# One fused transformer layer in float32: the rest of every second weight piece made by ScalarE and an accumulating DMA, and attention on unsplit float32

## The chip, the cores and the metric

The kernel runs on one core of a Trainium2 chip. The metric is the device time of one execution in microseconds (us). The engines are named as the profile names them: PE (TensorE, matrix products; PEld are its weight loads), DVE (VectorE), ACT (ScalarE), POOL (GpSimd) and SP (SyncE, which here only issues DMAs). SBUF is the on-chip memory of 128 partitions, PSUM the banks into which PE writes.

## The reference

One layer for 256 tokens of 2048 features. A mixer has two branches: dilated attention with three groups of 8 heads, and a gated linear attention. Both read one wide product of x; a gated sum of them goes through w_out, then comes a layer norm, a convolutional feed-forward block of 5632 features, and a second layer norm.

```
parts = split(x @ w_in)                       # q, k, v of three groups; gla inputs; gates
for each group: p = softmax(q k^T / sqrt(128) + bias), o = p v     # 8 heads of 128
ya = softmax-weighted sum of the groups' o, @ w_proj_a
yb = (gla(...) normalised * silu(gr)) @ w_proj_b
x  = layernorm(ALPHA x + (sigmoid(m_a) ya + sigmoid(m_b) yb) @ w_out)
h  = silu(conv3(x @ w_gate)) * (x @ w_up)
x  = layernorm(ALPHA x + h @ w_down)
```

All of it is float32, and nearly all of the time is matrix products with weights that are used once.

## The kernel before, in words

The weights come as a stream of pieces, each 128 partitions by 2048 float32 numbers (1 MB), which the host has laid out in the order of use. `piece` (line 135) takes the next one: SP loads it into a tile `raw` (three buffers), ACT copies it into a tile `whi` of type float32r, the main part (line 115), and DVE subtracts to get the rest, `wlo = raw - whi` (line 116); the kernel's comment calls the two exact 12-bit parts. `whi` and `wlo` have two buffers each.

Every product with the weights is made of three of such parts: main by main, main by rest, rest by main. Two forms of product use the pieces. `b_tile` (lines 182 to 189) makes 128 features by 256 tokens: for each of 16 blocks one matmul of 512 columns (line 187, both parts of the tokens against `whi`) and one of 256 (line 188, against `wlo`). `a_chunk` makes 128 tokens by 512 features with three matmuls of 512 columns for each block and half of the tokens (lines 237 to 239). A piece feeds 12288 streamed columns in either form. After a `b_tile`, `b_sum` (ACT line 231, DVE line 232) adds the two halves of the PSUM bank.

The order on each engine is set by a scheduler at build time, which lets ACT, DVE and SP work on pieces ahead of PE as far as the buffers allow. Every engine then executes its own list strictly in order; waits are on semaphores. So what an engine may do early is bounded by its list and by buffers: the next `whi` and `wlo` can be written only when PE has read the piece that held the buffer.

Around the stream the stages are: v, q and k of the attention heads with the attention itself pushed in between (`side`, `pump`), the linear attention's inputs, the linear attention, the projection `yp`, the gates `gr` and `m` with `pb`, `wo` with the first layer norm, and the feed-forward block with `fg` and `fu` (gate and up) and `wd` (down) in three parts of 20, 20 and 4 feature tiles.

Attention works on split operands: q and k are summed into a temporary tile and split (48 times), v is split on its way out of PSUM, and so are the transposed probabilities `pT`. `scores` (line 325) then takes two matmuls per half of the queries and two DVE operations to add the two PSUM halves and the bias; `mix` (line 366) takes four matmuls per group. The bias of a head is loaded by four small DMAs on POOL's queue (line 323) into a tile of the pool `big`, which has 7 buffers.

Of the kernel before, what the change touches and what calls it, by code (L numbers as in the profile page):

```python
# [14 lines left out]
ALU = mybir.AluOpType  # L15
# [22 lines left out]
# columns of w_in  # L38
# [8 lines left out]
# columns of the packed per-partition parameters  # L47
# [10 lines left out]
def hybrid_layer(ctx: ExitStack, tc: tile.TileContext, wp, xt, wgl, gw, par, relb, onehot, ln2, out):  # L58
# [20 lines left out]
    def blk(name, dt=F32):  # L79
        """2 KB of every partition."""  # L80
        n_blk[0] += 1
        return bpool.tile([P, 512], dt, tag="blk", name=f"{name}_{n_blk[0]}", bufs=NBLK)

    def tmp(name, dt=F32):
        """1 KB of every partition."""
        n_blk[0] += 1
        return tpool.tile([P, S], dt, tag="tmp", name=f"{name}_{n_blk[0]}", bufs=NTMP)

    def big(name, shape, dt=F32):
        """3 KB of every partition."""  # L90
        n_blk[0] += 1
        return tpool.tile([P, *shape], dt, tag="big", name=f"{name}_{n_blk[0]}", bufs=7)
# [25 lines left out]
    def piece_in_blocks(i, on_pool=None):  # L118
        """A piece out of turn, or one that leaves the pool's parts to the next."""
# [61 lines left out]
    def b_tile(name, parts, opnd, nk):  # L181
        """[128 features, tokens]: main part in columns :S, the rest in S:."""
# [13 lines left out]
    def b16_three(names, opnd, second):  # L196
        """Three feature tiles side by side, for an operand that is still being made."""
# [15 lines left out]
    def halves(a):  # L213
        return a.rearrange("p (a c) -> p a c", a=2)

    def evacuate(name, pss, parts=False):
        """[tile of tokens], or [tile of tokens][part]"""
        out = []
        for ps in pss:
            if parts:  # L220
                two = blk(name, F32R), blk(name, F32R)
                split(*two, ps)
                out.append(two)
            else:
                out.append(blk(name))
                nc.scalar.activation(out[-1], ps, AF.Copy)
# [14 lines left out]
    def a_chunk(name, opnd, nk, first=None, n_pump=1):  # L241
        """[128 tokens, 512] for both halves of the tokens."""
# [11 lines left out]
    def a_pair_by_half(name, opnd, second):  # L254
        """Two chunks of one piece each: first all of one half of the tokens."""
# [48 lines left out]
    def copies():  # L304
        """Every row once for each of 32 queries, so that a row's start can move with the query."""
# [8 lines left out]
    def attend(h, qk, vs, hp, hv):  # L314
        """Stages of head h: hp its place in its q and k tiles, hv in its v tiles."""
# [10 lines left out]
        def scores(g):  # L326
            def f():
                if not g:
                    st["s"] = blk("s0")[:, :384], big("s1", (768,))
                q, k = (x[hp] for x in qk[g])  # L330
                for t in range(2):
                    n = (t + 1) * P
                    ps = bank("ps")
                    nc.tensor.matmul(ps[:, : 2 * n], q[:, t * P : (t + 1) * P], halves(k)[:, :, :n], start=True, stop=False)
# [18 lines left out]
        def turn(g):  # L353
            def f():
# [6 lines left out]
                p = big("pT", (2, 384), F32R)  # L361
                split(p[:, 0], p[:, 1], pt[:, :384])
# [3 lines left out]
        def mix(g):  # L366
            def f():
                if not g:
                    st["po"] = bank("po")
                po, p = st["po"], st["p", g]  # L370
                v0, v1 = ([a[:, hv * P : (hv + 1) * P] for a in vs[g][t]] for t in range(2))
# [3 lines left out]
                nc.tensor.matmul(po[:, S + P :], v1[1], p[:, 0, S:], start=False, stop=(g == 2))  # L375
                if g == 2:
                    f32 = tmp("yaf")
                    b_sum(po, f32)
                    y = blk("ya", F32R)
                    split(y[:, :S], y[:, S:], f32)  # L380
# [9 lines left out]
    for half in range(2):  # L390
        vs = []
        for g in range(3):
# [5 lines left out]
            vs.append(evacuate("v", pss, parts=True))  # L398
        for pr in range(2):
            qk = []  # L400
            st = [attend(4 * half + 2 * pr + j, qk, vs, j, 2 * pr + j) for j in range(2)]
            for g in range(3):
                two = []
                for which in range(2):
                    hl = []
                    for j in range(2):
                        ps = b16("qk", xop)
                        f = tmp("qkf")
                        b_sum(ps, f)
                        hl.append(blk("qk", F32R))  # L410
                        split(hl[j][:, :S], hl[j][:, S:], f)
                        pump()
                    two.append(hl)
# [18 lines left out]
    # low-rank gate  # L432
# [5 lines left out]
    # both operands of the gate's product three times over, from rows 0, 32 and 64, so that  # L438
    # one pass over the rows sums the products of their parts
# [31 lines left out]
    def gla(h):  # L471
# [33 lines left out]
        def keys():  # L505
# [3 lines left out]
            # groups of two chunks of keys, for the chunks of queries 0 | 1 | 2, 3 | 2 | 3  # L509
# [141 lines left out]
    def residual(d):  # L651
        """ALPHA x, less the centre."""
# [162 lines left out]
NBLK = 38  # L815
NTMP = 14


# [1 line left out]
def _by_rows(w, c, n):  # L820
    """Columns c..c+n of all rows, 128 rows to a partition's place."""
# [46 lines left out]
def _bucket_rows():  # L868
    """One-hot buckets of the distance 255 - j, by group; a last row of -1e30 where it is masked."""
# [62 lines left out]
```

## Time and profile before

| | |
|---|---|
| two timed runs | 1923.16 and 1927.13 us, median 1925.14 |
| the profiled execution | 1924.5 us from its first to its last instruction; no other time is given for it, so what lies around the span is inside the 0.6 us between this and the median |
| granted clock of PE | 0.995 of full speed |
| busy: PE / DVE / ACT / POOL | 99% / 60% / 47% / 5% of the span |
| moved by DMA | 352.6 MB, mean 183 GB/s |

The page has a row per engine with its busy time, forty slices of the span with the busy tenths of each engine, and the chain of work that ended last. A group's row gives the source line, the engine, output and inputs, their shapes, the count, then busy us and the mean ns of one, then the idle time just before them and who ended it. A row of DMA issues ends with the median us from issue to landing.

### The profile page before, as it was taken

To read this page: it belongs to the slowest core of one execution; us is meant where nothing else is said; L and a number is where in the kernel's file an instruction comes from. 1 tells how busy PE (TensorE), PEld (TensorE's weight loads), DVE (VectorE), ACT (ScalarE), POOL (GpSimd) and SP (SyncE) were. 2 spreads that over 40 slices of the span, in tenths; PEclk is the share of its full clock that TensorE was granted. 3 is DMA by queue.
4 is the path that set the end of the run, shared out by engine and by line. 5 is a ranking of instruction groups with operands and counts; after the bars stand their busy time and mean duration, and the time that the engine had idled before them with its cause. 6 is when DMAs were issued, how large, how long until landed. Compare 5 with 4: busy or idle time off the path is not lost.

```text
span 1924.5 us, 24582 instructions
## 1 busy us (share of the span) xinstructions
PE 1897.7 (99%) x10208; PEld 1622.0 (84%) x10208; DVE 1154.3 (60%) x1324; ACT 900.1 (47%) x1084; POOL 104.4 (5%) x130
## 2 busy tenths in 40 slices
PE   9999999999999999999999998999999999999997
PEld 6888888888878888888888887888888888888885
DVE  5466565755656556655555757666654566664557
ACT  5445444453445554544444545554533455544342
POOL 0000000001000000000000452000000000000001
PEclk9999999999999999999999999999999999999998
DMA  7645545455544355555555553455555645555552
GB/s 273 231 178 175 191 175 182 166 191 175 180 154 145 140 191 182 194 178 195 177 193 179 197 192 114 176 190 182 190 186 195 239 180 192 181 191 200 198 194 86
DMA packets 56058, 352.60 MB, mean 183 GB/s; under 512 B 6737, under 2 KB 7660, under 8 KB 15500
## 3 DMA queue, kind: packets, MB, share of 16 engines
q1 hardware_dynamic: 53340, 345.10, 50.0%
q0 software_dynamic: 2464, 5.69, 1.0%
q8 instruction: 80, 1.31, 0.3%
q10 hardware_dynamic: 144, 0.26, 0.0%
q14 instruction: 30, 0.25, 0.0%
HBM read 348.85 MB, written 3.31 MB: 183 GB/s over the span
## 4 chain that ended last, share of the span: by engine, by line
PE 95%; DVE 3%; ACT 1%; issue 1%; DMA 1%; SPq 0%; DVEq 0%; ACTq 0%
PE qk L187 9%; PE fu L187 8%; PE fg L187 8%; PE m L187 6%; PE qk L188 5%; PE fu L188 4%; PE fg L188 4%; PE wd_t L238 4%; PE wd_t L237 4%; PE wd_t L239 4%; PE m L188 3%; PE pb L187 3%; PE gr L187 3%; PE gqk L187 3%; PE wo L187 2%; PE v_t L237 2%
## 5 line engine op out<-in xcount | busy, mean ns | idle before, releaser
L116 DVE TENSOR_TENSOR wlo<-raw,whi 128x2048 fp32r<-128x2048 f32 (+1 forms) x339 | 740.8, 2188 | 597.9 <-ACT whi L115 597.6
L115 ACT ACTIVATE whi<-raw 128x2048 fp32r<-128x2048 f32 (+1 forms) x339 | 617.4, 1824 | 454.7 <-issue 114.0
L187 PE MATMUL qk<-x,whi 128*128 128x512 f32 x768 | 273.8, 400 | 0.0
L187 PE MATMUL fu<-x,whi 128*128 128x512 f32 x688 | 244.9, 398 | 0.0
L187 PE MATMUL fg<-x,whi 128*128 128x512 f32 x672 | 239.7, 399 | 0.0
L188 PE MATMUL qk<-x,wlo 128*128 128x256 f32 x768 | 215.7, 281 | 0.0
L188 PE MATMUL fu<-x,wlo 128*128 128x256 f32 x688 | 193.2, 281 | 0.0
L188 PE MATMUL fg<-x,wlo 128*128 128x256 f32 x672 | 188.7, 281 | 0.0
L187 PE MATMUL m<-x,whi 128*128 128x512 f32 x512 | 181.7, 399 | 0.0
L187 PEld LDWEIGHTS qk<-x,whi 128*128 128x128 f32 x768 | 144.3, 188 | 35.3
L187 PEld LDWEIGHTS fu<-x,whi 128*128 128x128 f32 x688 | 129.2, 188 | 32.1
L187 PEld LDWEIGHTS fg<-x,whi 128*128 128x128 f32 x672 | 126.3, 188 | 31.0
L188 PEld LDWEIGHTS qk<-x,wlo 128*128 128x128 f32 x768 | 145.1, 189 | 0.0
L188 PE MATMUL m<-x,wlo 128*128 128x256 f32 x512 | 143.8, 281 | 0.0
L238 PE MATMUL wd_t<-wlo,h 128*128 128x512 f32 x344 | 134.1, 390 | 0.0
L239 PE MATMUL wd_t<-whi,h 128*128 128x512 f32 x344 | 133.9, 389 | 0.0
L237 PE MATMUL wd_t<-whi,h 128*128 128x512 f32 x344 | 133.7, 389 | 0.0
L188 PEld LDWEIGHTS fu<-x,wlo 128*128 128x128 f32 x688 | 130.0, 189 | 0.0
L188 PEld LDWEIGHTS fg<-x,wlo 128*128 128x128 f32 x672 | 127.0, 189 | 0.1
L187 PEld LDWEIGHTS m<-x,whi 128*128 128x128 f32 x512 | 96.2, 188 | 24.1
L188 PEld LDWEIGHTS m<-x,wlo 128*128 128x128 f32 x512 | 96.7, 189 | 0.0
L187 PE MATMUL pb<-ob,whi 128*128 128x512 f32 x256 | 91.1, 398 | 0.0
(251 smaller groups left out, 2991.5 us busy)
## 6 DMA issues: line engine op xcount, KB each, us to landing
raw<-in_wp SPq DMA_DIRECT2D x316, 1024.0 KB, 4.8
raw<-in_wp SPq DMA_DIRECT2D x24, 256.0 KB, 5.1
bias<-bvd POOLq DMA_DIRECT2D x32, 96.0 KB, 2.7
xraw<-in_xt SPq DMA_DIRECT2D x8, 256.0 KB, 5.2
braw<-in_wp SPq DMA_DIRECT2D x8, 256.0 KB, 5.0
ln<-in_ln POOLq DMA_DIRECT2D x8, 256.0 KB, 5.0
out<-acc SPq DMA_DIRECT2D x7, 256.0 KB, 2.5
bvd<-bvs SPq DMA_DIRECT2D x1, 1152.0 KB
```

The lines of the kernel that those rows point to most:

```text
L115: nc.scalar.activation(hi, src, AF.Copy)
L116: engine.tensor_tensor(lo, src, hi.bitcast(F32), op=ALU.subtract)
L187: nc.tensor.matmul(ps, hi, xo, start=(kc == 0), stop=False)
L188: nc.tensor.matmul(ps[:, S:], lo, xo[:, :S], start=False, stop=(kc == nk - 1))
L237: nc.tensor.matmul(ps, xh, hi, start=first, stop=False)
L238: nc.tensor.matmul(ps, xh, lo, start=False, stop=False)
L239: nc.tensor.matmul(ps, xl, hi, start=False, stop=last)
```

## The change

**Weight pieces.** For every piece with an even number that is loaded in one cut, DVE no longer makes the rest. ACT copies `raw` into `whi` as before (now line 144), copies `whi` with a scale of -1 into `wlo` (line 145), and POOL issues a DMA that adds the unsplit weights to `wlo` in place (line 146), so that `wlo = raw - whi` again. For numbers divisible by four the DMA reads the weights from memory a second time, for the other even ones from the tile `raw`. 158 pieces of the stream are made so, 79 of each kind. `whi` and `wlo` get three buffers each in place of two.

**Attention.** q, k, v and the probabilities stay whole float32 tiles. `scores` takes one plain float32 matmul per half of the queries, `mix` two per group; the splits and the second DVE addition go. `evacuate` only copies.

**Buffers.** `big` goes from 7 to 4, `NBLK` from 38 to 35, `NTMP` from 14 to 12.

```diff
     def big(name, shape, dt=F32):
-        return tpool.tile([P, *shape], dt, tag="big", name=f"{name}_{n_blk[0]}", bufs=7)
+        return tpool.tile([P, *shape], dt, tag="big", name=f"{name}_{n_blk[0]}", bufs=4)
...
     def piece(before=(None,)):
         i = n_piece[0]
         n_piece[0] += 1
         raw = wpool.tile([P, 2048], F32, tag="raw", name=f"raw_{i}", bufs=3)
-        hi = wpool.tile([P, 2048], F32R, tag="whi", name=f"whi_{i}")
-        lo = wpool.tile([P, 2048], F32R, tag="wlo", name=f"wlo_{i}")
+        hi = wpool.tile([P, 2048], F32R, tag="whi", name=f"whi_{i}", bufs=3)
+        lo = wpool.tile([P, 2048], F32R, tag="wlo", name=f"wlo_{i}", bufs=3)
+        if len(before) == 1 and i % 2 == 0:
+            nc.sync.dma_start(raw, wp[i])
+            nc.scalar.activation(hi, raw, AF.Copy)
+            nc.scalar.activation(lo, hi.bitcast(F32), AF.Copy, scale=-1.0)
+            nc.gpsimd.dma_start(lo, raw if i % 4 else wp[i], accum_op=ALU.add)
+            return hi, lo
...
-    def evacuate(name, pss, parts=False):
+    def evacuate(name, pss):
...
+            out.append(blk(name))
+            nc.scalar.activation(out[-1], ps, AF.Copy)
...
                 for t in range(2):
                     n = (t + 1) * P
-                    ps = bank("ps")
-                    nc.tensor.matmul(ps[:, : 2 * n], q[:, t * P : (t + 1) * P], halves(k)[:, :, :n], start=True, stop=False)
-                    nc.tensor.matmul(ps[:, n : 2 * n], q[:, S + t * P : S + (t + 1) * P], k[:, :n], start=False, stop=True)
+                    pt = ps[:, t * P : t * P + n]
+                    nc.tensor.matmul(pt, q[:, t * P : (t + 1) * P], k[:, :n], start=True, stop=True)
                     s = st["s"][t][:, g * n : (g + 1) * n]
-                    for part, rest in ((ps[:, n : 2 * n], st["T"][:, g, S - n :]), (ps[:, :n], s)):
-                        nc.vector.scalar_tensor_tensor(s, part, scale, rest, op0=ALU.mult, op1=ALU.add)
+                    nc.vector.scalar_tensor_tensor(s, pt, scale, st["T"][:, g, S - n :], op0=ALU.mult, op1=ALU.add)
...
-                nc.tensor.matmul(po, v0[0], p[:, :, :S], start=(g == 0), stop=False)
-                nc.tensor.matmul(po[:, S:], v0[1], p[:, 0, :S], start=False, stop=False)
-                nc.tensor.matmul(halves(po)[:, :, P:], v1[0], p[:, :, S:], start=False, stop=False)
-                nc.tensor.matmul(po[:, S + P :], v1[1], p[:, 0, S:], start=False, stop=(g == 2))
+                nc.tensor.matmul(po, v0, p[:, :S], start=(g == 0), stop=False)
+                nc.tensor.matmul(po[:, P:], v1, p[:, S:], start=False, stop=(g == 2))
...
-NBLK = 38
-NTMP = 14
+NBLK = 35
+NTMP = 12
```

How the order moves is shown at three places. The first is ACT in the feed-forward block. Names are tile names with a running number; a row's brackets name the engine or DMA queue whose semaphore it waits for (DMAHW: a DMA issued by SP, DMASW: one issued by POOL). Before, four pieces' main parts in a row of ACT's list, with what stands between them (`pa` is the first half of `b_sum`, `sg` and `gr` belong to the gate, `h` is the split of the product):

```order
L115 ACTIVATE whi_10754<-raw_10753 128x2048 [waits DMAHW2_49,PE_49,Activation_49]
L762 ACTIVATE sg_10656<-gr_10652 128x256 [waits DVE_49]
L231 ACTIVATE pa_10698<-fu_10664 128x256 [waits PE_49]
L115 ACTIVATE h_10702<-yb_10697 128x256 [waits DVE_49]
L115 ACTIVATE whi_10801<-raw_10800 128x2048 [waits DMAHW3_49,PE_49,Activation_49]
L231 ACTIVATE pa_10744<-fg_10711 128x256 [waits PE_49]
L758 ACTIVATE gr_10747<-gbuf_96,prm 128x256 [waits DVE_49]
L115 ACTIVATE whi_10849<-raw_10848 128x2048 [waits DMAHW4_49,PE_49,Activation_49]
```

Now, at the same kind of place: the main part of an even piece, `whi_10091`, its turned copy `wlo_10092`, and the main part of the odd piece that follows, `whi_10140`:

```order
L229 ACTIVATE pa_9926<-fg_9893 128x256 [waits PE_49]
L746 ACTIVATE gr_9929<-gbuf_98,prm 128x256 [waits DVE_49]
L144 ACTIVATE whi_10091<-raw_10090 128x2048 [waits DMAHW3_49,PE_49]
L750 ACTIVATE sg_9933<-gr_9929 128x256 [waits DVE_49]
L229 ACTIVATE pa_9975<-fu_9941 128x256 [waits PE_49]
L145 ACTIVATE wlo_10092<-whi_10091 128x2048 [waits DMASW7_49,Activation_49]
L115 ACTIVATE h_9979<-yb_9974 128x256 [waits DVE_49]
L717 ACTIVATE acc_9457<-pback_9982 128x512 [waits PE_49]
L115 ACTIVATE whi_10140<-raw_10139 128x2048 [waits DMAHW4_49,PE_49]
```

The turned copy is a second row of 2048 columns per even piece, behind `sg` and `pa`; `pa_9975` reads the product of the piece three before. Of the 158 turned copies 41 have `sg` and `pa` between them and their main part, 31 have nothing, and nearly all of the others one row of 256 or 384 columns.

The second place is the queue of loads, SP's list, in the same stretch (`raw_10090` is the even piece above, `raw_10037` and `raw_10139` the odd ones around it). Before, every load waits for a subtraction of DVE:

```order
L147 DMA raw_10705<-in_wp 128x2048 [waits DMAHW6_49,DVE_49]
L147 DMA raw_10753<-in_wp 128x2048 [waits DMAHW7_49,DVE_49]
```

Now, in SP's list and then in POOL's:

```order
L153 DMA raw_10037<-in_wp 128x2048 [waits DMAHW7_49,Activation_49]
L143 DMA raw_10090<-in_wp 128x2048 [waits DMAHW0_49,DVE_49]
L153 DMA raw_10139<-in_wp 128x2048 [waits DMAHW1_49,DMASW1_49,Activation_49]
L143 DMA raw_10192<-in_wp 128x2048 [waits DMAHW2_49,DVE_49]
L153 DMA raw_10241<-in_wp 128x2048 [waits DMAHW3_49,Activation_49]
```

```order
L146 DMA wlo_9888<-in_wp 128x2048 [waits DMASW3_49,DVE_49,Activation_49]
L146 DMA wlo_9990<-raw_9988 128x2048 [waits DMASW6_49,DVE_49,DMAHW1_49,PE_49,Activation_49]
L146 DMA wlo_10092<-in_wp 128x2048 [waits DVE_49,DMASW7_49,PE_49,Activation_49]
L146 DMA wlo_10194<-raw_10192 128x2048 [waits DMASW0_49,DVE_49,DMAHW5_49,PE_49,Activation_49]
```

One load in four (`raw_10139`) now waits for an accumulating DMA, the one that read its buffer before (`wlo_9990<-raw_9988`); the loads of the next pieces stand behind it in SP's list. POOL's list, which had nothing between the first layer norm and the DMAs of the last part of the feed-forward block, has an accumulating DMA for every second piece.

The third place is PE in the attention stage. The scores of a head and group, before and now:

```order
L334 MATMUL ps_920<-qk_721,qk_629 128x256
L335 MATMUL ps_920<-qk_721,qk_629 128x128
L334 MATMUL ps_925<-qk_721,qk_629 128x512
L335 MATMUL ps_925<-qk_721,qk_629 128x256
```

```order
L333 MATMUL ps_892<-qk_578 128x128
L193 MATMUL qk_903<-x_80,whi_898 128x512 [waits DVE_49,Activation_49]
L194 MATMUL qk_903<-x_80,wlo_899 128x256 [waits DVE_49]
L193 MATMUL qk_903<-x_80,whi_898 128x512
L333 MATMUL ps_892<-qk_578 128x256 [waits DVE_49]
```

Four float32r matmuls have become two plain float32 ones, with matmuls of the weight stream between them.

More of the change, by code (lines that the diff above doesn't have):

```diff
@@ L211, in b16_three @@
         return pss
-    def halves(a):
-        return a.rearrange("p (a c) -> p a c", a=2)
-    def evacuate(name, pss, parts=False):
+    def evacuate(name, pss):
         out = []
         for ps in pss:
[L220 to L226, printed above, removed]
+            out.append(blk(name))
+            nc.scalar.activation(out[-1], ps, AF.Copy)
         return out
@@ L360, in f @@
                     nc.tensor.transpose(pt[:, (kt + 1) * P : (kt + 2) * P], s1[:, c : c + P], ident)
-                p = big("pT", (2, 384), F32R)
-                split(p[:, 0], p[:, 1], pt[:, :384])
+                p = blk("pT")[:, :384]
+                nc.scalar.activation(p, pt[:, :384], AF.Copy)
                 st["p", g] = p
@@ L368, in f @@
                 if not g:
[L369 removed]
+                    st["po"] = bank("po")[:, :S]
                 po, p = st["po"], st["p", g]
[L371 to L375 removed]
+                v0, v1 = (vs[g][t][:, hv * P : (hv + 1) * P] for t in range(2))
+                nc.tensor.matmul(po, v0, p[:, :S], start=(g == 0), stop=False)
+                nc.tensor.matmul(po[:, P:], v1, p[:, S:], start=False, stop=(g == 2))
                 if g == 2:
[L377 to L378 removed]
                     y = blk("ya", F32R)
[L380 removed]
+                    split(y[:, :S], y[:, S:], po)
                     YA[h] = y
@@ L402, in hybrid_layer @@
             for g in range(3):
-                two = []
+                two = [blk("qk") for _ in range(2)]
                 for which in range(2):
-                    hl = []
                     for j in range(2):
                         ps = b16("qk", xop)
[L408 to L411, printed above, removed]
+                        b_sum(ps, two[j][:, which * S : (which + 1) * S])
                         pump()
-                    two.append(hl)
                 qk.append(two)
```

5 lines of the change are left out of this document (3 added, 2 removed).

## The prediction

> **What bounds the kernel now.** I read the page first: busy times, the slices with PE's clock, and the chain that ended last.
>
> ```profile
> PE 1897.7 (99%) x10208; PEld 1622.0 (84%) x10208; DVE 1154.3 (60%) x1324; ACT 900.1 (47%) x1084; POOL 104.4 (5%) x130
> PEclk9999999999999999999999999999999999999998
> PE 95%; DVE 3%; ACT 1%; issue 1%; DMA 1%; SPq 0%; DVEq 0%; ACTq 0%
> q1 hardware_dynamic: 53340, 345.10, 50.0%
> raw<-in_wp SPq DMA_DIRECT2D x316, 1024.0 KB, 4.8
> ```
>
> PE is busy in 99% of the span at its full clock and is 95% of the chain. All else hides behind it. So 1924.5 - 1897.7 = 26.8 us is all that better cover could win, 1.4%; a larger gain needs less work on PE. Next, the timeline of PE, ACT and SP in the feed-forward block, to get the beat of the stream.
>
> ```profile
> 1302.63 0.40 PE L187 MATMUL fu<-x,whi 128*128 128x512 f32 x1
> ...
> 1308.28 0.40 PE L187 MATMUL fg<-x,whi 128*128 128x512 f32 x1
> ```
>
> ```profile
> 1308.41 1.92 ACT L115 ACTIVATE whi<-raw 128x2048 fp32r<-128x2048 f32 x1 [0.44 <-PE fu L187]
> 1310.23 0.40 ACT L762 ACTIVATE sg<-gr 128x256 f32<-128x256 f32 x1
> 1310.54 0.37 ACT L231 ACTIVATE pa<-fu 128x256 f32<-128x256 f32 x1
> ```
>
> A piece lasts 1308.28 - 1302.63 = 5.65 us on PE, a pair 11.3. ACT starts the next main part 0.13 us after PE has begun another piece, since only then is a buffer free (it ended its wait on PE, `fu`). The pieces are made just in time, and making one takes ACT and then DVE in this order:
>
> ```profile
> L116 DVE TENSOR_TENSOR wlo<-raw,whi 128x2048 fp32r<-128x2048 f32 x315 | 723.1, 2296 | 593.4 <-ACT whi L115 593.1
> L115 ACT ACTIVATE whi<-raw 128x2048 fp32r<-128x2048 f32 x315 | 603.3, 1915 | 446.0 <-issue 110.7 <-PE wd_t L239 94.4 <-PE v_t L239 45.1
> ```
>
> That is 1.9 + 2.3 = 4.2 us from a free buffer to a ready piece. With two buffers it has one piece's time, 5.65, so it fits with 1.4 to spare. Everything below asks whether the new way fits.
>
> **The change: engine time.** How full ACT and DVE are in one pair:
>
> ```profile
> 1300.00:1311.30 11.30, 11.30 (x65) 9.80 (x64) 7.07 (x9) 5.70 (x7) 0.00 (x0) 1.00 0.54 187
> ```
>
> In these columns (after the length: PE, PEld, DVE, ACT, POOL, clock, DMA share, GB/s) DVE has 7.07 of 11.3 us and loses 2.3; ACT has 5.70 and gains 1.9, so 7.6. Both still fit and cost nothing by their load. The splits and additions that attention loses on ACT and DVE were covered by PE, and are worth nothing.
>
> **The change: attention on PE.** The scores of one head and group, and a plain float32 product that the kernel already has (two passes of 256 columns, then two of 128):
>
> ```profile
> 116.33 0.28 PE L334 MATMUL ps<-qk,qk 128*128 128x256 f32 x1
> ...
> 116.92 0.40 PE L187 MATMUL qk<-x,whi 128*128 128x512 f32 x1
> ```
>
> ```profile
> 658.02 0.60 PE L558 MATMUL pgo<-att,gv 128*128 128x256 f32 x2
> 658.46 0.39 PE L559 MATMUL pgo<-att,gv 128*128 128x128 f32 x2
> 658.68 0.60 PE L558 MATMUL pgo<-att,gv 128*128 128x256 f32 x2
> ```
>
> Scores took 116.92 - 116.33 = 0.59 us. Now they are one float32 matmul of 256 columns (658.46 - 658.02 = 0.44) and one of 128 (0.22), 0.66. A `mix` streams as many columns as scores, 512 + 256 + 256 + 128; at 5.65 us for 12288 columns that is 0.53, and now 0.66 too. 24 x (0.07 + 0.13) = 5 us more on PE; no sign of a gain (bounds 3 to 7).
>
> **The change: the rest of a piece.** An even piece now takes ACT twice and then a DMA. By the new order its main part waits, through its buffer, for the end of the piece three before (call that moment E), and PE needs the rest two pieces later, at E + 11.3. ACT's part: the main part starts at E + 0.13, the next row 1.82 later, `pa` 0.31 after that, a third row another 0.31. So the turned copy ends at 0.13 + 1.82 + 1.92 = 3.9 with nothing between, 4.2 with one row, 4.5 with `sg` and `pa`. Weighted with 31, 86 and 41 places: 4.2. This leaves 7.1 us for the DMA.
>
> No accumulating DMA is in the trace, so its price is bounded. A load of the same size lands 4.8 us after its issue. How much of that is flow: 345.10 MB take 50.0% of the span, so a 1.05 MB piece takes 0.0030 x 962 = 2.9 us; and in the DMA slices of the window 1300 to 1325 (0.625 us each)
>
> ```profile
> GB/s 13 0 0 105 157 262 446 419 315 0 0 0 131 79 275 419 419 341 13 0 0 105 92 249 419 419 393 0 0 0 92 144 210 419 433 380 0 0 0 0
> ```
>
> the rate stands at 419 where it is steady, which gives 2.5. I take 2.7, with 2.1 fixed (1.0 before the flow, 1.1 after). POOL's own DMAs have the same fixed part:
>
> ```profile
> glr<-in_wgl POOLq DMA_DIRECT2D x1, 128.0 KB, 2.3
> ln<-in_ln POOLq DMA_DIRECT2D x8, 256.0 KB, 5.0
> ```
>
> 128 KB are 0.3 us of flow, so 2.0. An accumulating DMA must read what is in `wlo` beside the weights, then write. Lower bound: the flow c of a plain copy, 2.7. Two reads in a row: 5.4. Two reads and the write in a row: 8.1. I take 5.4, as it moves two streams in where a load moves one, and the write of a load already runs beside its read.
>
> The Trainium skill says the same of a reduce (Collectives: The Full Stack, "Part 3", "The bandwidth ceiling"): the addition is free, but two source reads make it half as fast as a copy; no run here shows it yet. With that page's 31 GB/s per engine, an estimate of c is 2 x 1.05 MB / (16 x 31 GB/s) = 4.2 us, and the sum below would end at 2025.
>
> Alone, the DMA would take 2.1 + 5.4 = 7.5 against 7.1: almost fitting. But it isn't alone. The `ln` rows show a POOL DMA of 256 KB landing after 5.0 us in the stream, 2.2 more than 2.1 fixed and 0.7 of flow: it stands behind loads on the same DMA engines. And the new order bunches the loads. One load in four waits for the accumulating DMA that reads its `raw` buffer; SP's list is in order, so the next load, long free to go, waits behind it, and the third is free as soon as the following even piece's main part is copied. Three loads, 8.1 us of flow, start together, and the next accumulating DMA, one that reads memory, falls into them.
>
> Count from L, where the DMA that frees the buffer lands, and X = L + e, where PE takes up the piece that it completed. The three loads flow from L + 1.0 to L + 9.1. The next even piece's E is X, or a little before; its DMA is issued at X + 4.2 and flows from X + 5.2. Loads still to flow: R = 9.1 - 5.2 - e = 3.9 - e, and if both share, the DMA lands R later: at X + 5.2 + 5.4 + R + 1.1 = X + 11.7 + R. PE wanted it at X + 11.3, so it stands for s = 0.4 + R. The even piece after that reads `raw`, with no bunch in its way; its DMA lands at X + 11.3 + 4.2 + 7.5 = X + 23.0, and PE comes for it at X + 22.6 + s, so e = s - 0.4. Together: s = 0.4 + 3.9 - (s - 0.4), s = 2.35 us per four pieces. For any c this is s = c - 3.05. There are 79 such fours: 79 x 2.35 = 186 us.
>
> POOL's other work goes in the same list. In the `wo` stage its two additions per piece stand ahead of the DMA:
>
> ```profile
> L688 POOL TENSOR_TENSOR s<-s,sg 128x256 f32<-128x256 f32 x14 | 27.5, 1964 | 3.8 <-ACT sg L685 3.7
> L687 POOL TENSOR_TENSOR s<-s,r 128x256 f32<-128x256 f32 x14 | 15.7, 1120 | 42.2 <-DVE r L683 42.2
> L323 POOL DMA_DIRECT2D bias<-bvd x32 | 17.4, 550 | 425.6 <-PE po L375 365.0 <-DMA bvd<-bvs 49.2 <-PE ppt L360 11.4
> ```
>
> They take 3.1 us, where ACT's part takes 4.2, so mostly side by side: 0 to 25 us over 8 even pieces. The `bias` DMAs used to wait 365 us for attention's buffers, at no cost, with nothing behind them. Now accumulating DMAs stand behind them, and `big` is smaller; the new order has them later, so 0 to a piece (5.65) for each of three groups, 17. I take 4 for both.
>
> Sum on the profiled execution: 1924.5 + 5 + 186 + 4 = 2120 us. Its span is 0.6 below the median of the runs, which changes nothing. Base 1933.5, and 79 us for each us of c above 3.05.
>
> **The rivals.** *The accumulating DMA costs what a copy costs* (not slower). If the second read runs beside the first, c is 2.7, the DMA takes 4.8 alone, s is below zero and the stream never stands: 1933 us, 0.5% more. It decides up to c = 3.4. For it: the slices show DMA engines idle for nearly half of the time. Against it: at 419 GB/s the flow of a load already looks limited, and twice the data must come in. Chance 0.17.
>
> *The loads don't bunch or don't share.* Then R = 0, s = 0.4 at c = 5.4 and 0 at 5.0: 1965 us, 2.1% more, or 1934. For it: the loads are small against the gaps in the slices. Against it: the `ln` row. By the Trainium skill's rule (DMA: Bandwidth & Descriptors, "Issuing engines are not separate DMA queues") the DMAs of all issuers interleave on the same 16 engines; the `ln` row agrees. Chance 0.13.
>
> *The addition is slow.* At c = 10.8, four loads' worth, the DMA engines themselves are the bound: four loads and two accumulating DMAs are 10.8 + 21.6 = 32.4 us per four pieces against 22.6, so 79 x 9.8 = 774 more: 2710 us. Up to c = 8.1 my chain decides (2332), from there on this. Nothing in the trace speaks for or against it but that no addition was ever seen there. Chance 0.17.
>
> That the change doesn't do what it says is excluded by POOL's order, which holds the 158 DMAs.
>
> **How the numbers follow.** My forecast, waits of PE for the accumulating DMA, with c between 4 and 8.1, has 0.50 and its own range is 2010 to 2330. The rest, 0.03, is unforeseen. Two per cent, about what a measurement can tell from no change, is 1963.6. Within 2%: 0.17, about half of the second rival, 0.07, and 0.03 of the rest, 0.27. Faster by 2% would need 38 us, more than PE's 26.8 idle, with more PE work: 0.01. Slower: 0.72. The range for 8 in 10 starts at the first rival's 1930, and ends at 2330, leaving out the slow addition and a little below.
>
> **What would show it.** In the changed profile, PE's busy share falls to near 90%, and the waits list has PE or PEld of the `wlo` lines waiting for the DMA into `wlo`, about once per four pieces, 1 to 3.5 us each, and mostly for the one that reads memory. Issue to landing of `wlo<-in_wp` is above that of `wlo<-raw`, which is near 7.5. SP's loads come in threes in the slices. PE's clock stays 9. Were the first rival right, both land in about 5 us and PE keeps 99%. Were the slow addition right, the DMA slices stand at 9 all through, and every even piece is waited for. I'd be wrong as well if the waits of PE were for ACT's turned copy.

## The result, and the profile after

| | before | after |
|---|---|---|
| timed runs, median | 1925.14 us | 2238.91 us (2238.82 and 2239.00) |
| ratio | | 1.163, interval 1.160 to 1.167 |
| span of the profiled execution | 1924.5 us | 2237.1 us |
| mean granted clock of PE | 0.995 | 0.950 |
| PE busy | 1897.7 us | 1983.9 us |
| PE idle (span less busy) | 26.8 us | 253.2 us |

The kernel became 16% slower. The forecast was 2120 us with a range of 1930 to 2330. The direction and the mechanism of the waits came out, and the time lies in the range, 119 us above the value; most of these 119 us are a term that the prediction put at nothing, the clock.

The page of the kernel after, in the rows that answer to those shown of before (busy times, PE's clock and the DMA engines in forty slices, the chain, the DMA queues and issues):

```profile
PE 1983.9 (89%) x10208; PEld 1677.6 (75%) x10208; DVE 751.6 (34%) x1026; ACT 1159.3 (52%) x1186; POOL 232.6 (10%) x288
PEclk8899999999999999999999998999999999999999
DMA  9688888887877788888888765888878888888884
q1 hardware_dynamic: 53340, 345.10, 41.7%
q0 software_dynamic: 25216, 171.37, 38.2%
PE 47%; DMA 34%; issue 15%; ACT 2%; DVE 1%; POOL 1%; POOLq 0%; SPq 0%
raw<-in_wp SPq DMA_DIRECT2D x316, 1024.0 KB, 4.9
wlo<-in_wp POOLq DMA_DIRECT2D x79, 1024.0 KB, 9.9
wlo<-raw POOLq DMA_DIRECT2D x79, 1024.0 KB, 7.0
```

PE has gone from 99% to 89%, and a third of the chain is now DMA; the DMA engines are busy for 7 to 9 tenths of most slices. An accumulating DMA that reads the `raw` buffer lands after 7.0 us, one that reads memory after 9.9. Who waits for them, in the list of waits (total us, times, longest):

```profile
PE fg L194 <- DMA wlo<-in_wp: 63.8, 21, 7.2
PE v_t L236 <- DMA wlo<-in_wp: 28.4, 4, 13.4
PE wo L194 <- DMA wlo<-raw: 2.1, 1, 2.1
SPq L153 <- DMA wlo<-raw: 932.9, 73, 15.2
```

Over all lines, the rows of PE waiting for a DMA into `wlo` add up to 225.6 us in 81 waits: 219.7 us in 75 waits on the kind that reads memory, 5.9 us in 6 on the other. PE's idle time grew by 253.2 - 26.8 = 226.4 us, so these waits are all of it. PE's busy time grew by 1983.9 - 1897.7 = 86.2 us too, with the same 10208 matmuls; where that comes from is seen below.

One wait, in order of time, in the feed-forward block (start, duration, then in brackets the idle time ahead and who ended it). `wlo<-raw` and `wlo<-in_wp` on POOL are the two kinds of accumulating DMA; SP's rows are loads; ACT L144 and L145 are the main part and the turned copy:

```profile
1529.16 0.87 POOL L146 DMA_DIRECT2D wlo<-in_wp  x1 [18.00 <-ACT h L115]
1534.39 0.33 SPq L143 DMA_DIRECT2D raw<-in_wp  x1
1537.37 0.39 PE L194 MATMUL fg<-x,wlo 128*128 128x256 f32 x1 [1.39 <-DMA wlo<-in_wp]
1540.25 0.87 POOL L146 DMA_DIRECT2D wlo<-raw  x1 [10.22 <-ACT h L115]
1547.16 0.33 SPq L153 DMA_DIRECT2D raw<-in_wp  x1
1547.58 0.38 SPq L143 DMA_DIRECT2D raw<-in_wp  x1
1548.62 1.92 ACT L144 ACTIVATE whi<-raw 128x2048 fp32r<-128x2048 f32 x1 [0.44 <-PE fu L193]
1550.57 0.33 SPq L153 DMA_DIRECT2D raw<-in_wp  x1
1551.01 1.91 ACT L145 ACTIVATE wlo<-whi 128x2048 fp32r<-128x2048 f32 x1
1553.21 0.86 POOL L146 DMA_DIRECT2D wlo<-in_wp  x1 [12.09 <-ACT h L115]
1564.07 0.39 PE L194 MATMUL fg<-x,wlo 128*128 128x256 f32 x1 [3.83 <-DMA wlo<-in_wp]
```

The raw kind is issued at 1540.25; the load that waits for its buffer goes out at 1547.16, 6.9 us later, which is its landing. Two more loads follow within 3.4 us. The memory kind is issued at 1553.21 behind these three and lands 10.9 us later, when PE has stood for 3.83 us. The memory kind before it, at 1529.16, had no such bunch ahead and landed after 8.2 us; PE stood for 1.39. What the DMA engines moved meanwhile, in slices of 0.625 us from 1540 to 1565:

```profile
GB/s 52 0 210 210 210 210 210 210 210 210 0 0 0 210 170 433 446 419 446 446 419 406 419 419 419 354 92 105 118 210 223 197 210 210 210 262 380 433 433 302
```

Eight slices at 210 are the raw kind alone: 5.0 us for 1.05 MB, half the 419 of the loads that follow.

### The profile page after: what moved, and what is told of

It reads as the page before. It is cut to its first block, busy times and chain, and to the rows that moved or that the text cites. A ratio compares the mean times of both kernels' runs of the same rounds, so it can differ in the third digit from the quotient of the medians.

```text
span 2237.1 us, 25028 instructions
## 1 busy us (share of the span) xinstructions
PE 1983.9 (89%) x10208; PEld 1677.6 (75%) x10208; DVE 751.6 (34%) x1026; ACT 1159.3 (52%) x1186; POOL 232.6 (10%) x288
## 4 chain that ended last, share of the span: by engine, by line
PE 47%; DMA 34%; issue 15%; ACT 2%; DVE 1%; POOL 1%; POOLq 0%; SPq 0%
DMA wlo<-in_wp 34%; PE qk L193 4%; PE fg L193 4%; PE fu L193 3%; PE m L193 3%; PE qk L194 2%; PE fg L194 2%; PE wd_t L236 2%; PE gqk L193 2%; PE wd_t L237 2%; PE wd_t L235 2%; PE fu L194 2%; PE m L194 2%; PE v_t L236 1%; PE pb L193 1%
## 5 line engine op out<-in xcount | busy, mean ns | idle before, releaser
L116 DVE TENSOR_TENSOR wlo<-raw,whi 128x2048 fp32r<-128x2048 f32 (+1 forms) x181 | 378.2, 2094 | 855.0 <-ACT whi L115 854.4
L115 ACT ACTIVATE whi<-raw 128x2048 fp32r<-128x2048 f32 (+1 forms) x181 | 315.3, 1745 | 469.4 <-PE fg L193 134.7
L144 ACT ACTIVATE whi<-raw 128x2048 fp32r<-128x2048 f32 x158 | 302.1, 1912 | 268.5 <-PE qk L193 86.6
L145 ACT ACTIVATE wlo<-whi 128x2048 fp32r<-128x2048 f32 x158 | 301.1, 1906 | 1.0
L193 PE MATMUL fg<-x,whi 128*128 128x512 f32 x672 | 261.7, 425 | 0.0
L194 PE MATMUL fg<-x,wlo 128*128 128x256 f32 x672 | 202.6, 301 | 63.8 <-DMA wlo<-in_wp 63.8
L194 PEld LDWEIGHTS fg<-x,wlo 128*128 128x128 f32 x672 | 139.7, 208 | 70.7 <-DMA wlo<-in_wp 70.7
L146 POOL DMA_DIRECT2D wlo<-in_wp x79 | 68.7, 870 | 1091.2 <-ACT wlo L145 570.7
L193 PEld LDWEIGHTS fg<-x,whi 128*128 128x128 f32 x672 | 138.4, 206 | 33.0
L146 POOL DMA_DIRECT2D wlo<-raw x79 | 68.7, 870 | 796.7 <-ACT wlo L145 506.4
```

The source lines that it names most:

```text
L115: nc.scalar.activation(hi, src, AF.Copy)
L116: engine.tensor_tensor(lo, src, hi.bitcast(F32), op=ALU.subtract)
L144: nc.scalar.activation(hi, raw, AF.Copy)
L145: nc.scalar.activation(lo, hi.bitcast(F32), AF.Copy, scale=-1.0)
L146: nc.gpsimd.dma_start(lo, raw if i % 4 else wp[i], accum_op=ALU.add)
L193: nc.tensor.matmul(ps, hi, xo, start=(kc == 0), stop=False)
```

## Experiments

All ratios are against the kernel before on the same chip. "Waits" is the sum of PE's waits for DMAs into `wlo`, with their count.

| | median us | ratio (interval) | waits us (count) | PE busy us | landing us, memory / raw kind |
|---|---|---|---|---|---|
| after | 2238.91 | 1.163 (1.160 to 1.167) | 225.6 (81) | 1983.9 | 9.9 / 7.0 |
| e1, attention only | 1925.61 | 1.003 (1.001 to 1.004) | none | 1900.8 | |
| e2, a quarter, memory | 2093.74 | 1.090 (1.088 to 1.092) | 125.2 (66) | 1934.8 | 8.2 / - |
| e3, a quarter, raw | 1978.27 | 1.031 (1.029 to 1.032) | 34.7 (30) | 1914.0 | - / 6.9 |
| e4, all from memory | 2119.69 | 1.104 (1.102 to 1.106) | 144.2 (93) | 1947.8 | 8.2 / - |
| e5, all from raw | 2280.27 | 1.188 (1.183 to 1.192) | 244.2 (127) | 2004.2 | - / 11.2 |
| e6, copy | 1988.53 | 1.035 (1.031 to 1.040) | 48.3 (30) | 1909.1 | 6.8 / 4.2 |
| e7, main part first | 2027.90 | 1.055 (1.053 to 1.058) | 75.7 (54) | 1916.7 | 12.8 / 8.2 |
| e8, fill | 2206.25 | 1.148 (1.144 to 1.152) | 96.2 (49) | 2075.6 | 10.0 / 6.9 |
| e9, four raw buffers | 2248.69 | 1.170 (1.167 to 1.173) | 224.8 (79) | 1986.8 | 10.1 / 7.2 |
| e10, its control | 2249.42 | 1.170 (1.167 to 1.173) | 231.3 (81) | 1987.5 | 10.1 / 7.2 |
| e11, main first, all memory | 1951.82 | 1.015 (1.012 to 1.018) | 22.2 (9) | 1891.6 | 10.3 / - |
| e12, main first, a quarter raw | 1924.99 | 1.001 (1.000 to 1.002) | 4.5 (3) | 1891.0 | - / 6.9 |

The theory was the prediction's: PE waits for accumulating DMAs that are too long for the 7.1 us that the order leaves them, above all for one that falls among bunched loads. The rivals were reading memory twice, the DMA engines' throughput, and the attention.

**e1: attention alone.** Every piece is made in the old way.

```diff
-        hi = wpool.tile([P, 2048], F32R, tag="whi", name=f"whi_{i}", bufs=3)
-        lo = wpool.tile([P, 2048], F32R, tag="wlo", name=f"wlo_{i}", bufs=3)
-        if len(before) == 1 and i % 2 == 0:
+        hi = wpool.tile([P, 2048], F32R, tag="whi", name=f"whi_{i}", bufs=2)
+        lo = wpool.tile([P, 2048], F32R, tag="wlo", name=f"wlo_{i}", bufs=2)
+        if False:
```

> Attention on whole float32 with the smaller buffers, weight pieces as before (ACT, then DVE, two buffers). My theory, that the loss is in the weight pieces: 1930 us, 5 us more than before, PE busy near 1903 us. Rival, that a good part of the loss is attention (plain float32 matmuls, fewer buffers): 1950 us or more.

The median is 1925.61 against 1919.16 on its chip; by the ratio about 5 us more. PE's busy time rises by 1900.8 - 1897.7 = 3.1 us. The attention's share is settled at the predicted 5; all else comes from the pieces.

**e2 and e3: half of the accumulating DMAs, of one kind only.** e2 keeps those that read memory, e3 those that read `raw`.

```diff
-        if len(before) == 1 and i % 2 == 0:
+        if len(before) == 1 and i % 4 == 0:
```

> Only every fourth piece is made with an accumulating DMA, always from memory; the other even pieces are made by DVE. No load waits for an accumulating DMA any more. Theory (the DMA from memory falls into three loads that start together): loads stay spaced, the DMA lands after 7 to 8.5 us in place of 9.9, and the time is 1930 to 2000 us, likeliest 1950. Rival (the second read of memory is slow in itself): it still lands near 9.9 us, PE waits near 2.9 us 79 times with the clock falling, 2180 us or more.

```diff
-        if len(before) == 1 and i % 2 == 0:
+        if len(before) == 1 and i % 4 == 2:
```

> Only every fourth piece is made with an accumulating DMA, always from the tile raw; the other even pieces are made by DVE. Loads still wait for it and start together, but no accumulating DMA falls into them. Theory: it lands in 7.0 us, PE does not wait, 1935 us. Rival (an accumulating DMA is late by itself wherever it reads, or POOL's list is): waits of 1 us or more per four pieces, 2010 us or more.

The landings came as the theory had them: without loads waiting for a raw-reading DMA the memory kind lands in 8.2 us instead of 9.9. The times did not: e2 lost 174 us and e3 59, and each lies between its theory and its rival. For e2 the theory's time did not follow from its own landing: 8.2 us against the 7.1 that fit are 1.1 us in each of 79 pieces, 87 us, and the waits after the start measure 103.4. Two costs more were missing in the theory, and both are in the rows of e2: half clock (PE busy 1934.8, 34.0 over e1), and the start, where two waits in the v stage make 21.8 of the 125.2 us. e3 has 6.3 us there.

**e4 and e5: every even piece of one kind.**

```diff
-            nc.gpsimd.dma_start(lo, raw if i % 4 else wp[i], accum_op=ALU.add)
+            nc.gpsimd.dma_start(lo, wp[i], accum_op=ALU.add)
```

> All 158 accumulating DMAs read memory, none the tile raw, so no load waits for one; a quarter more is read from memory. Theory (bunched loads are the cause): each overlaps one load at most and lands after 8 to 8.5 us, PE waits near 0.6 us per pair, 2030 us (1950 to 2090). Rival (reading memory is the cause): landing 9.9 us or more for all 158, waits in every pair, 2250 us or more.

```diff
-            nc.gpsimd.dma_start(lo, raw if i % 4 else wp[i], accum_op=ALU.add)
+            nc.gpsimd.dma_start(lo, raw, accum_op=ALU.add)
```

> All 158 accumulating DMAs read the tile raw, none memory; now every second load waits for one, and the load behind it with it. Theory (bunched loads): bunches of two, each accumulating DMA meets about 1 us of them and lands after 8 us, PE waits near 0.45 us per pair, 2005 us. Rival (reading memory is the cause): all land in 7.0 us and PE does not wait, 1935 us.

Two turns of e5's timeline (SP's loads, POOL's accumulating DMA, PE behind its wait):

```profile
1541.00 0.33 SPq L153 DMA_DIRECT2D raw<-in_wp  x1
1541.42 0.38 SPq L143 DMA_DIRECT2D raw<-in_wp  x1
1543.27 0.86 POOL L146 DMA_DIRECT2D wlo<-raw  x1 [11.36 <-ACT h L115]
1555.16 0.39 PE L194 MATMUL fg<-x,wlo 128*128 128x256 f32 x1 [1.08 <-DMA wlo<-raw]
1555.17 0.33 SPq L153 DMA_DIRECT2D raw<-in_wp  x1
1555.59 0.38 SPq L143 DMA_DIRECT2D raw<-in_wp  x1
```

This pair decides between bunching and memory traffic as the larger cost. e4 reads more from memory than the kernel after and is faster, 1.104 against 1.163; e5 reads no piece twice and is slower. In e5 a load waits for every accumulating DMA, two loads leave the moment one lands (1555.17), and the next falls into both: 11.2 us where the same kind alone takes 6.9. So the long landings follow the loads that stand just ahead. With every accumulating DMA reading memory, only 2 of the 93 that PE waited for had three or more loads near their issue.

Where the DMA reads counts too, though for less. Three of e4's DMAs (issued at 2024.28, 2074.19 and 2086.04) have no load issued in the 5 us ahead of them, and land after 8.2, 8.4 and 8.0 us; of the 474 that read memory in the kernel after, e2, e4 and e11 none lands under 7.76. The raw kind lands after 6.9 in e3, and of e6's plain copies the shortest land after 4.99 from memory and 4.08 from `raw`. Reading memory thus costs some 1.2 us by itself, and in the kernel after the bunch another 3.2 (8.2 against 11.4, see below).

In size the theory failed twice, with 2030 for e4 and 2005 for e5. Where every even piece is late, the wait for one gives the next as much more time, so by the prediction's chain the wait is half of 4.2 + landing - 11.3: 0.55 us in e4 and 2.05 in e5, times 158, which is 87 and 324. The waits outside the v stage are 144.2 - 29.0 = 115 and 244.2 - 18.0 = 226. So the chain gives the order of size when it is fed the landings that occur, and no better. For e5 the expectation had the landing too short, and both lacked the half clock: PE's busy time is 47 and 103 us above e1's.

**e6: the same DMA without the addition.**

```diff
-            nc.gpsimd.dma_start(lo, raw if i % 4 else wp[i], accum_op=ALU.add)
+            nc.gpsimd.dma_start(lo, raw if i % 4 else wp[i])
```

> The same DMAs on POOL's queue, but copying the weights into the tile of the rest and not adding them (the products with the rest are then other numbers). Theory (the second read is the price): one read flows in 2.5 us, the DMA lands in 5 us alone and below 7 among loads, PE does not wait, 1935 us. Rival (POOL's queue or the wait of the loads is the price, not the addition): landing and time as in the changed kernel, near 2240 us.

```profile
q0 software_dynamic: 25216, 171.37, 23.1%
wlo<-in_wp POOLq DMA_DIRECT2D x79, 1024.0 KB, 6.8
wlo<-raw POOLq DMA_DIRECT2D x79, 1024.0 KB, 4.2
```

Same DMAs, same queues, same packets. A copy from `raw` lands in 4.2 us where the addition took 7.0: 2.8 us for the addition with its second read, priced at 2.7; the run does not tell the two apart. It is worth 2238.91 - 1988.53 = 250 us. The time missed the 1935 us expected. Of the 66 that stay over before, 5 are the attention's; the list of waits has 48.3, of which 16.9 are two at the start.

**e7, e11, e12: give the DMA more time.** In a piece, all products with the main part come first, then those with the rest, so PE needs `wlo` later. Shown is the product of features by tokens; the other form is turned in the same way. e11 adds e4's edit, e12 e3's.

```diff
-            hi, lo = parts(kc)
-            xo = opnd(kc)
-            nc.tensor.matmul(ps, hi, xo, start=(kc == 0), stop=False)
-            nc.tensor.matmul(ps[:, S:], lo, xo[:, :S], start=False, stop=(kc == nk - 1))
+            nc.tensor.matmul(ps, parts(kc)[0], opnd(kc), start=(kc == 0), stop=False)
+        for kc in range(nk):
+            nc.tensor.matmul(ps[:, S:], parts(kc)[1], opnd(kc)[:, :S], start=False, stop=(kc == nk - 1))
```

> The changed kernel with each piece's matmuls in another order: all that read the main part first, then those that read the rest, which is then needed 3.7 us later. Theory (PE's wait for the accumulating DMA from memory is the whole loss but for attention): waits of 2.9 us go, the clock stays full, 1940 us. Rival (DMA engines are full and set the beat): the waits only move, 2100 us or more.

> Products with the main part first, and all 158 accumulating DMAs from memory, so that no load waits for one. Theory (what main first alone left, 2028 us, are the accumulating DMAs that meet the bunched loads): landings of 8.2 us are 1.1 us over what fits, and the rest is needed 3.7 us later, so no waits and a full clock: 1935 to 1950 us. Rival (the DMA engines, busy 86% of the time, are the bound once PE waits less): 2000 us or more.

> Products with the main part first, and only every fourth piece made with an accumulating DMA, from the tile raw. Theory: its landing of 6.9 us fits with 3.7 us to spare, no waits, 1926 to 1935 us, as attention alone. Rival (there is a cost of the accumulating DMA that is not PE's wait): near the 1978 us that it takes without the new order.

The issues of the memory kind in e7, then queues and issues of e11, then the chain of e12:

```profile
wlo<-in_wp POOLq DMA_DIRECT2D x79, 1024.0 KB, 12.8
```

```profile
q0 software_dynamic: 25216, 171.37, 46.7%
q1 hardware_dynamic: 53340, 345.10, 46.4%
wlo<-in_wp POOLq DMA_DIRECT2D x158, 1024.0 KB, 10.3
```

```profile
PE 92%; DVE 3%; DMA 2%; ACT 2%; issue 1%; POOL 0%; SPq 0%; ACTq 0%; POOLq 0%; DVEq 0%
```

e7 recovers 211 of the 314 us though its DMAs land later than ever (12.8 us): what counts is when PE comes for them. Its 2028 us lie between the 1940 expected and the rival's 2100. Most of what e7 still loses goes when no load waits for an accumulating DMA: e11 comes down to 1.5%, just above its 1935 to 1950, with the two queues' packets taking 93% of the DMA engines' time. So throughput isn't the bound. e12 is level with before, but two things cancel in it: PE's busy time is 9.8 us below e1's 1900.8, and its idle time is 10.4 above (34.9 against 24.5), of which 4.5 are waits for accumulating DMAs. So what else these DMAs cost in idle time of PE is at most some 6 us. No kernel here beats the one before. In e11 too PE's busy time is below e1's, by 9.2 us; whether the new order of the products alone would gain that was not run.

**e8: keep PE busy during the wait.** Ahead of the first product with a rest that was read from memory stand eight matmuls whose result nobody reads.

```diff
+    def fill(a, b):
+        late[0] = False
+        ps = bank("fill")
+        for _ in range(8):
+            nc.tensor.matmul(ps, a, b, start=True, stop=True)
...
+            if kc == 0 and late[0]:
+                fill(hi, xo)
```

> The changed kernel with eight extra matmuls of 512 columns (1.9 us, into a bank that nobody reads) on PE ahead of the first product that needs a rest from memory, so that the wait there holds no long idle time. Theory (after a wait PE runs some microseconds at half clock, which is the 81 us that PE's busy time grew beyond attention): the clock stays at 1.0 but the wait itself grows a little, 2170 to 2200 us. Rival (the clock costs nothing): 2240 us or more, since where the wait is short the extra matmuls add to it.

Adding work made it faster: 1.148 against 1.163, some 29 us. The 632 extra matmuls of 512 columns are 632 x 0.235 = 149 us of PE (5.65 us per 12288 columns). Without them PE's busy time is 2075.6 - 149 = 1927, 26 over e1 where after has 83. So waits fell by 129, clock losses by 57, and 149 were spent: -37, against -36.2 measured between the two spans. The time came just above the 2170 to 2200 expected, and the clock rose from 0.950 to 0.981, not to 1.0.

**e9 and e10: a fourth raw buffer.** It needs room, taken from other buffers; e10 is that alone.

```diff
-            raws = wpool.tile([P, 2048], F32, tag="raw", name=f"raw_{i}", bufs=3)
+            raws = wpool.tile([P, 2048], F32, tag="raw", name=f"raw_{i}", bufs=4)
...
-        raw = wpool.tile([P, 2048], F32, tag="raw", name=f"raw_{i}", bufs=3)
+        raw = wpool.tile([P, 2048], F32, tag="raw", name=f"raw_{i}", bufs=4)
...
-NBLK = 35
+NBLK = 31
```

> The changed kernel with four buffers of raw in place of three (and 31 blocks in place of 35, for the room). Sources and bytes stay; what changes is which load waits for an accumulating DMA: now an even piece's, four pieces on, with one load behind it that is free, so bunches of two and not three. Theory (bunched loads): the DMA from memory lands after 8 to 9 us in place of 9.9, the waits fall by about half, 2090 us (2030 to 2150). Rival (what counts is only the bytes on the DMA engines): as the changed kernel, 2220 us or more.

> The changed kernel with 31 blocks in place of 35 and nothing else, beside the run with four buffers of raw. Theory: blocks are not what it waits for, 2240 us. Rival: the smaller pool costs by itself, 2260 us or more.

The expectation for e9 fell: 2090 was forecast, and e9 equals its control. The control itself lies 0.6% above the kernel after, between its two expectations, so the smaller pool may cost a little. The longest wait of SP's queue (total us, times, longest), e9 and then e10:

```profile
SPq L143 <- DMA wlo<-raw: 922.8, 72, 14.5
```

```profile
SPq L153 <- DMA wlo<-raw: 926.0, 72, 15.2
```

The wait has not gone, it has moved by one load. The kinds of piece repeat every four, so with four buffers the load that takes the raw-reading DMA's buffer is again one of an even piece (L143), and it waits as often and as long. That the bunch depends on the ring as such is thus neither shown nor excluded; five buffers were not tried.

## Why the prediction was right, and what was mis-sized

**What bounds it, the attention, engine loads.** Right. e1 gives 5 us where 5 was said, 3.1 of them in PE's busy time. ACT at 52% and DVE at 34% are not the bound.

**The price of the DMA.** Right for the raw kind. Fixed 2.1 and c = 5.4 made 7.5 alone; it measured 7.0, with 5.0 of flow at half a load's rate. The prediction gave the memory kind the same price; it is some 1.2 us dearer, as e4 shows. The Trainium skill's rule on two source reads (Collectives: The Full Stack, Part 3, "The bandwidth ceiling") agrees with 210 against 419 GB/s; the estimate of c from its figure, 4.2, was too low.

**The bunch.** Right in kind, not in rhythm. The prediction had it in every four pieces, with one wait of 2.35 us. The trace has it in about every second of these fours: of the 75 memory kinds that PE waited for, 34 had three or more loads issued between 6.5 us before their own issue and 4 after (median landing 11.4 us, mean wait 3.8), and 41 had fewer (8.2 us, 2.2). After a long wait, as from 1553 on above, the next loads go out spread (1571.42, 1575.46, 1578.79), and the following DMA lands early. With PE hardly stopping, as in e7, the bunch is there nearly every time: 48 of 50 late ones had three or more loads. What the estimate left out is that even without a bunch the memory kind takes 8.2, not 7.0, and so misses its 7.1 us. Also, of the three loads the second is hardly held by SP's order: at 1547.58 it goes 0.4 us after DVE's subtraction set its buffer free. The bunch is as much a coincidence of two buffers as a queue. Without the start these waits are 225.6 - 23.7 = 201.9 us; predicted were 186. That the two are so near is partly luck: 128 us come from the 34 in a bunch and 68 from the 39 without one, where the chain had each of 79 in a bunch and the memory kind cheaper.

**PE's clock.** Wrong: "PE's clock stays 9". The waits were counted at their own length, but each longer one is paid a second time. Windows of 4 us behind waits of 1.39, 3.83 and 5.17 us (PE, PEld, DVE, ACT, POOL, then granted clock, DMA share, GB/s):

```profile
1537.47:1541.47 4.00, 4.00 (x24) 3.50 (x24) 1.27 (x3) 2.79 (x5) 0.87 (x1) 1.00 0.44 176
1564.17:1568.17 4.00, 4.00 (x15) 3.37 (x16) 0.42 (x1) 0.35 (x2) 0.86 (x1) 0.57 0.83 209
1617.13:1621.13 4.00, 4.00 (x10) 3.13 (x11) 0.00 (x0) 0.00 (x0) 0.00 (x0) 0.50 0.95 201
```

Behind a short wait the clock is whole and PE starts 24 matmuls in 4 us; behind the long ones it is at half for most or all of the window, with 15 and 10 (the 10 have 512 columns each, of which 17 would fit at 0.235 us). Of PE's 82 waits over 0.5 us, of any kind, 39 are followed by such a drop; one of them, 4.1 us behind DVE, is in both kernels. The busy time grew by 86.2 us, 3.1 of it the attention's; 83.1 / 38 is 2.2 us a drop. e8 shows the cause: with PE busy in the waits, 57 us of it go. The Trainium skill has the rule (TensorE: Matmul & The Clock Gate, Part 1: half clock behind an idle window of about 3.4 us, full clock after as long a busy one). It was not weighed in the prediction, where waits of 1 to 3.5 us were forecast, and it should have been a term there.

**ACT's part of 4.2 us.** Right in the stream: for the 128 even pieces whose main part waited for PE, the median from the end of that wait to the DMA's issue is 4.3 us. Wrong at the start. There the turned copy stands in ACT's list behind the copies of v out of PSUM, which wait for the end of the piece PE is on (rows of ACT, POOL and PE in order of time):

```profile
26.48 1.92 ACT L144 ACTIVATE whi<-raw 128x2048 fp32r<-128x2048 f32 x1 [2.13 <-DVE bv L298]
31.25 1.28 ACT L224 ACTIVATE v<-v_t 128x512 f32<-128x512 f32 x2 [2.85 <-PE v_t L237]
32.42 1.90 ACT L145 ACTIVATE wlo<-whi 128x2048 fp32r<-128x2048 f32 x1
34.63 0.91 POOL L146 DMA_DIRECT2D wlo<-in_wp  x1 [31.32 <-ACT wlo L145]
45.72 0.79 PE L236 MATMUL v_t<-wlo,x 128*128 128x512 f32 x1 [13.38 <-DMA wlo<-in_wp]
...
69.35 1.90 ACT L144 ACTIVATE whi<-raw 128x2048 fp32r<-128x2048 f32 x1
...
82.38 0.80 PE L236 MATMUL v_t<-wlo,x 128*128 128x512 f32 x1 [10.34 <-DMA wlo<-in_wp]
```

The main part ends at 28.40, the turned copy starts at 32.42, and by then PE has nothing left: it stands for 13.4 us. It stands again for 10.3 at 82.38; there the main part too (69.35) comes behind the copies of v (68.18). These two make 23.7 us. The prediction placed a late step in ACT only in its last sentence, as a way to be wrong. The late turned copy accounts for at most 4.0 of the first 13.4 us; the accumulating DMA itself takes 11.1 us there, from 34.63 to 45.72, with PE idle all through. That the order on ACT alone causes these waits was not tried apart.

**POOL's other work.** Predicted 4; POOL issues the DMA 0.3 us after the turned copy in all but 3 of 158 cases, and in those (at 654.7, 1203.6 and 1475.0) after 1.0 to 1.7 us. That is 3 us in all, inside the waits counted above.

**The sum again.** 1924.5 + 3.1 attention + 201.9 waits in the stream + 23.7 at the start + 83.1 half clock + 0.8 other = 2237.1, the span. Of the 117.6 us between this and the predicted sum of 2119.5, 83.1 are the clock, 23.7 the start, 15.9 the waits, 0.8 other idle time, and -1.9 and -4 the attention's and POOL's terms.

**The rivals.** Copy-priced: refuted by 7.0 against 4.2 in e6, though e6 shows that even then 3.5% would have been lost. No bunching or sharing: refuted by 8.2 against 11.4 us and by e4 against e5. Slow addition: refuted by 5.0 us of flow, and by e11, which has as many accumulating DMAs as the kernel after, all from memory, and loses 1.5%.

## What to carry to other kernels

An operation moved from an engine with room to a DMA must be priced from the free buffer to the landing, beside the loads that its own buffer waits will bunch, and not by the load it takes off the engine. PE at 99% has nothing to win from a less busy DVE, and a wait that idles PE for some 2 us of one 3.41 us window of its clock (last section) costs about 2 us more, 2.2 in the mean here. If such a DMA can't be made shorter, let PE ask for its result later: putting the products that don't need it first brought back 211 of 314 us, and once no load waited for such a DMA, all but 1.5% over the kernel before came back.

## What was not expected of the hardware

The clock falls behind waits much shorter than thought. Of PE's waits over 0.5 us in the kernel after, all 29 of 3.2 us or more were followed by half clock, none of the 34 below 1.75 was, and 10 of the 19 between were. The row of one of these, and windows of 0.5 us behind it (the clock is the third number from the end):

```profile
1772.09 0.39 PE L194 MATMUL fg<-x,wlo 128*128 128x256 f32 x1 [2.43 <-DMA wlo<-in_wp]
...
1772.00:1772.50 0.50, 0.41 (x2) 0.41 (x3) 0.47 (x2) 0.50 (x1) 0.00 (x0) 1.00 0.99 410
1773.00:1773.50 0.50, 0.50 (x3) 0.41 (x3) 0.00 (x0) 0.50 (x1) 0.00 (x0) 0.50 0.12 49
1776.00:1776.50 0.50, 0.50 (x4) 0.45 (x4) 0.00 (x0) 0.00 (x0) 0.00 (x0) 0.94 1.19 246
```

PE stood for 2.43 us, went on at full clock for half a microsecond, and then ran at half for some 3.4. The Trainium skill's page named above asks for an idle window of about 3.4 us; here 2.43, and in one place 1.75, were enough.

What decides between 1.75 and 3.2 can be read from the places of the drops. The 39 stretches of half clock in the trace begin at whole multiples of 3.413 us from each other, and last 3.41 us or multiples of it but for the last, which the end of the kernel cuts short. So the clock is set on a fixed grid of such windows, and what counts is how long PE was idle within one. A window of this grid with the one behind it, and then two windows with the one behind them:

```profile
707.67:711.09 3.42, 1.67 (x10) 1.13 (x8) 2.47 (x9) 3.20 (x6) 0.00 (x0) 1.00 0.97 287
711.09:714.50 3.41, 3.41 (x13) 2.84 (x11) 0.00 (x0) 1.63 (x1) 0.86 (x1) 0.50 0.37 132
...
1663.41:1666.83 3.42, 1.83 (x9) 1.17 (x7) 0.44 (x1) 1.78 (x1) 0.00 (x0) 1.00 0.98 204
1666.83:1670.24 3.41, 1.82 (x8) 1.52 (x9) 0.00 (x0) 2.04 (x2) 0.87 (x1) 1.00 0.89 341
1670.24:1673.65 3.41, 3.41 (x17) 2.83 (x16) 0.00 (x0) 0.00 (x0) 0.00 (x0) 1.00 0.94 192
```

The wait of 1.75 us lies within one window, and half clock follows. The wait of 3.18 us that ends at 1668.42 is split by the grid into 1.59 and 1.59, and the clock stays whole. Over the kernel after, from PE's first matmul to its last and in windows at full clock, half clock followed all 36 with 1.98 us or more of PE's idle time, 2 of the 7 with 1.58 to 1.98, and none of the 543 with less. The clock came back after each of the 38 windows at half clock in which PE was idle for less than 0.6 us, and after none of the other 24.
